# Writing the SSD skip term into the output banks with ScalarE ahead of the products

## The chip, the cores and the metric

One core of a Trainium2 chip. The metric is the device time of one execution in microseconds, and the median over runs is compared. TensorE (PE in the profile) multiplies matrices into PSUM banks of 128 x 512 float32; VectorE (DVE), ScalarE (ACT) and GpSimd (POOL) work elementwise; SyncE (SP) issues most of the transfers.

## The reference

A hybrid decoder layer on 1024 tokens of width 1024, float32: a Mamba-2 SSD branch and a latent-attention branch from one input projection, merged by gates, then a gated feed-forward part. The change is in the SSD mixer. With 32 heads of 64 channels, 4 groups of 8 heads, a state of 128 and chunks of 128 tokens it computes

```python
y_diag = jnp.einsum('bcgls,bcgels,bcsgep->bclgep', scores, decay_in, xc)      # within a chunk
y_off = jnp.einsum('bclgn,cbgepn,bcgel->bclgep', cc, prev, jnp.exp(a_cum))    # from the carried state
...
y = ssd_chunked_scan(xs * dt[..., None].astype(xs.dtype), dt * a, bm, cm)     # y_diag + y_off
y = y + xs * d_skip[:, None]                                                  # the skip term
y = y.reshape(b, l, D_INNER) * jax.nn.silu(z)                                 # the gate
y = rms_norm(y.reshape(b, l, SSD_GROUPS, D_INNER // SSD_GROUPS), ...)
```

## The kernel before

**Stages.** The profile's span begins with the norm and small projections, then attention (to about 703 us), then the SSD stage, the output projections of both branches, the up projection and the down projection. Large products are done three times, as float32r high and low parts (`mm3`, L175 to L177: high x high, high x low, low x high); the operands are split by a ScalarE cast (L153, L146) and a subtraction (L154, L148) on GpSimd or VectorE.

**The SSD stage.** It walks over 4 groups `g` of 8 heads and, within a group, over 8 chunks `c` of 128 tokens. Data lie with channels on partitions: `chan[g]` (tile `xg`) is 128 x 4 x 1024, four blocks `j` of 128 channels (two heads each). For each group:

- `conv_group` projects B, C and x of the group (`conv_tile`: matmuls into `lin` banks, eviction to `craw` by ScalarE at L808, convolution by ScalarE at L810 and three VectorE steps at L812, then silu at L816 and L817). It runs as background work for the next group.
- `ssd_inputs(g, c)` prepares a chunk: transposes of x and B (`xp`, `sp`), the decay matrix `seg` (ScalarE: eight L850, then L852; VectorE L864 multiplies the scores on), `xdt`, `xde` and `bt` (L855, L860, L863), and for c > 0 the decayed C in `abc` (ScalarE L866, VectorE L867).
- `ssd_state(g, c)` forms the chunk's state (`sn`, L874) and carries it on (`st`: GpSimd L879, VectorE L881).
- `ssd_output(g, c)` forms the output transposed in one bank `yp` of 128 x 512: for each block j two products of 64 channels x 128 tokens with `seg` (L891, which start their sums), and for c > 0 two with `st` and `abc` (L896, which add to them). Then it issues the load of the next chunk's gate (`z_load`, tile `zt`, on GpSimd's queue, L796), and VectorE adds the skip term block by block (L903, four of 128 x 128) and multiplies with the gate (L905, 128 x 512). The result stays in place in `chan[g]`.
- `ssd_squares` (L914 to L916) and `ssd_finish` norm the group's channels (`np_`, `grr`) and write them to memory.

**Order.** `ssd_steps` yields in the order: state c, inputs c+1, output c. Between two yields `advance` places a counted number of background steps (each one `mm3`) among TensorE's instructions: the convolution of the next group, the z projections (`z_tiles`, evicted by L329 and L330), in the last group the attention branch's output projection (`mla_tiles`, evicted by VectorE at L1033, with splits of its inputs at L146 and L148). These use two `lin` banks in turn. TensorE keeps the order as written. For ScalarE, VectorE and GpSimd in this stage a list planner sets the order of each engine's queue when the program is built, by the written order and its own estimates of when operands are ready; a few splits are tied behind the instruction written before them (`ordered_split`). On the chip each queue runs in order.

**Buffers.** `yp` and `seg` and `zt` have two buffers each, `abc` three; `xp`, `sp`, `sn` and `np_` one bank each; with the two `lin` banks and two `yp` banks all eight banks are in use. `hds` holds half of `d_skip` per channel; the projected activations carry a factor of two from the form of silu that is used, which the halves take out.

## Time and profile before

| | |
|---|---|
| time, median of 3 runs (lowest to highest) | 2197.95 us (2196.79 to 2203.98) |
| profiled execution: time, span | 2203.12 us, 2201.3 us |
| granted TensorE clock, mean | 0.996 |
| busy: PE, DVE, ACT, POOL | 97%, 66%, 48%, 44% |
| first and last L891 | 803.0, 1242.6 us |

A share of busy time is a mean over stages. In the rows of a group the numbers are count, busy time in us, mean ns of one instruction, and the idle time just before these instructions with what ended it. In a timeline row they are the start, the length in us, the engine, the line, the operation with its tiles, and in brackets the idle time ahead of it and its releaser. A row of a list of waits gives total us, how often, and the longest. A row of stretches gives the length and then each engine's busy time with its instruction count.

### The profile page before, as it was taken

To read this page: it belongs to the slowest core of one execution; us is meant where nothing else is said; L and a number is where in the kernel's file an instruction comes from. 1 tells how busy PE (TensorE), PEld (TensorE's weight loads), DVE (VectorE), ACT (ScalarE), POOL (GpSimd) and SP (SyncE) were. 2 spreads that over 40 slices of the span, in tenths; PEclk is the share of its full clock that TensorE was granted. 3 is DMA by queue.
4 is the path that set the end of the run, shared out by engine and by line. 5 is a ranking of instruction groups with operands and counts; after the bars stand their busy time and mean duration, and the time that the engine had idled before them with its cause. 6 is when DMAs were issued, how large, how long until landed. Compare 5 with 4: busy or idle time off the path is not lost. (4 is left out here: it accounts for less than half of the span.)

```text
span 2201.3 us, 30448 instructions
## 1 busy us (share of the span) xinstructions
PE 2145.3 (97%) x10844; PEld 1713.8 (78%) x10844; DVE 1446.8 (66%) x2567; ACT 1064.3 (48%) x2034; POOL 969.6 (44%) x1049
## 2 busy tenths in 40 slices
PE   8999999999999999999999999999899999999999
PEld 7877776777777887778877787887678888877787
DVE  4466756575664469898877746545876676676762
ACT  5445454555454456656564424324655455554330
POOL 2344424432443237665456311013377777744430
PEclk9999999999999999999999999999999999999999
DMA  4221111111112224645266566542132333248642
GB/s 147 69 69 46 40 53 64 50 35 55 64 48 88 93 82 148 195 151 172 92 229 212 178 224 200 166 161 95 63 119 92 111 105 110 96 138 330 258 158 82
DMA packets 121767, 268.97 MB, mean 122 GB/s; under 512 B 13520, under 2 KB 25744, under 8 KB 121616
## 3 DMA queue, kind: packets, MB, share of 16 engines
q1 hardware_dynamic: 105600, 214.47, 29.0%
q0 software_dynamic: 14528, 49.29, 6.8%
q10 hardware_dynamic: 1488, 3.28, 0.4%
q8 instruction: 85, 1.39, 0.3%
q14 instruction: 66, 0.54, 0.1%
HBM read 201.45 MB, written 65.54 MB: 121 GB/s over the span
## 5 line engine op out<-in xcount | busy, mean ns | idle before, releaser
L175 PE MATMUL lin<-h,whi 128*128 128x512 f32 x1440 | 591.6, 411 | 1.5 <-DVE lt L330 1.5
L177 PE MATMUL lin<-h,wlo 128*128 128x512 f32 x1440 | 563.7, 391 | 0.0
L176 PE MATMUL lin<-h,whi 128*128 128x512 f32 x1440 | 562.4, 391 | 0.0
L175 PEld LDWEIGHTS lin<-h,whi 128*128 128x128 f32 x1440 | 270.6, 188 | 83.9 <-issue 33.8
L177 PEld LDWEIGHTS lin<-h,wlo 128*128 128x128 f32 x1440 | 270.4, 188 | 59.8 <-POOL wlo L154 0.4
L176 PEld LDWEIGHTS lin<-h,whi 128*128 128x128 f32 x1440 | 271.5, 189 | 53.2 <-issue 6.7
L154 POOL TENSOR_TENSOR wlo<-wraw,whi 128x512 fp32r<-128x512 f32 x134 | 193.0, 1458 | 169.3 <-ACT whi L153 165.7
L153 ACT CAST whi<-wraw 128x512 fp32r<-128x512 f32 x232 | 141.1, 619 | 260.0 <-PE lin L176 111.1
L664 POOL TENSOR_TENSOR acc<-acc,e 128x512 f32<-128x512 f32 (+3 forms) x80 | 78.8, 984 | 246.1 <-ACT e L659 223.7
L659 ACT ACTIVATE e<-s 128x512 f32<-128x512 f32 (+1 forms) x192 | 93.3, 492 | 153.7 <-DVE s L657 133.1
L1140 DVE TENSOR_TENSOR xlo<-ur,xhi 128x512 fp32r<-128x512 f32 (+1 forms) x41 | 83.0, 2024 | 60.9 <-ACT xhi L1139 60.9
L154 DVE TENSOR_TENSOR wlo<-wraw,whi 128x512 fp32r<-128x512 f32 x98 | 70.0, 725 | 75.1 <-ACT whi L153 74.7
L850 ACT ACTIVATE seg<-abc,acum 128x128 f32<-128x128 f32 x256 | 80.2, 390 | 47.1 <-PE yp L891 41.0
L175 PE MATMUL dps<-tq,h 128*128 128x512 f32 x242 | 96.8, 400 | 5.8 <-DVE xr L1601 3.5
L176 PE MATMUL dps<-tq,h 128*128 128x512 f32 x242 | 96.9, 400 | 0.8 <-DVE tq L154 0.8
L177 PE MATMUL dps<-tq,h 128*128 128x512 f32 x242 | 96.4, 398 | 0.0
L812 DVE SCALAR_TENSOR_TENSOR xg<-craw,cl,xg 128x1024 f32<-128x1024 f32 x48 | 73.7, 1536 | 27.4 <-ACT xg L810 26.9
L664 DVE TENSOR_TENSOR acc<-acc,e 128x512 f32<-128x512 f32 (+3 forms) x80 | 55.1, 689 | 37.1 <-ACT e L659 36.5
L1216 POOL DMA_DIRECT2D mt<-m_d x16 | 8.6, 539 | 147.1 <-DVE gt L1225 97.1
L154 DVE TENSOR_TENSOR h<-ar,h 128x1024 fp32r<-128x1024 f32 (+1 forms) x35 | 56.4, 1616 | 25.4 <-ACT h L153 25.3
L670 PE MATMUL pv<-e,vt 128*64 128x512 f32 (+3 forms) x384 | 72.9, 498 | 0.0
L629 DVE CUSTOM_DVE_ANT_0 s<-s,negw 128x128 f32<-128x128 f32 (+3 forms) x128 | 62.3, 495 | 13.5 <-PE s L627 13.4
(617 smaller groups left out, 5225.7 us busy)
## 6 DMA issues: line engine op xcount, KB each, us to landing
wraw<-in_w_main SPq DMA_DIRECT2D x112, 256.0 KB
ur<-in_w_up SPq DMA_DIRECT2D x44, 512.0 KB
ar<-f_d SPq DMA_DIRECT2D x34, 512.0 KB
abc<-ac_d POOLq DMA_DIRECT2D x32, 512.0 KB, 5.3
wraw<-in_w_ssd SPq DMA_DIRECT2D x64, 256.0 KB
f_d<-wraw POOLq DMA_DIRECT2D x33, 256.0 KB, 2.4
g_d<-lt SPq DMA_DIRECT2D x32, 256.0 KB
z_d<-lt SPq DMA_DIRECT2D x32, 256.0 KB
```

Of the source, the lines that this page charges most:

```text
L153: S.copy(hi, raw)
L154: (eng or V).tensor_sub(lo, raw, hi.bitcast(F32))
L175: PE.matmul(ps, lhsT=ah, rhs=bh, start=first, stop=False, **more)
L176: PE.matmul(ps, lhsT=ah, rhs=bl, start=False, stop=False, **more)
L177: PE.matmul(ps, lhsT=al, rhs=bh, start=False, stop=last, **more)
L629: V.tensor_tensor_reduce(ps[:, 0:w], ps[:, 0:w], negw[:, 512 - w:512], 1.0, 2 * NEG, ALU.add, ALU.max, nm[:, j, i:i + 1])
L659: S.activation(e[:, c0:512], ps[:, 0:w], AF.Exp)
L664: (V if hd else G).tensor_tensor(accs[hd][:, c0:512], accs[hd][:, c0:512], e[:, c0:512], op=ALU.add)
L670: PE.matmul(pv[hd * 64:(hd + 1) * 64, c0:512], lhsT=vt[:, j, hd * 64:(hd + 1) * 64], rhs=es[hd][:, c0:512], start=first, stop=last)
L812: V.scalar_tensor_tensor(c, raw[:, k:k + T], col(cw + k), c, op0=ALU.mult, op1=ALU.add)
L850: S.activation(seg[:, hd, :], abc[:, hd, :], AF.Relu, bias=acum[:, c, 8 * g + hd:8 * g + hd + 1], scale=-1.0)
L1140: eng.tensor_sub(lo, r, hi.bitcast(F32))
```

## The change

`yp` is now taken at the end of `ssd_inputs`, and ScalarE writes the skip term into it there (x of the chunk times `hds`, four copies of 128 x 128 with a per-partition scale). The products of `ssd_output` no longer start their sums; all of them add to what the bank holds. Three new matmuls of 128 x 512, which do start their sums, write the two `yp` banks in full before the first chunk (the first bank twice). VectorE's four L903 are gone, and its last operation reads the bank and the gate and writes `chan[g]`.

```diff
@@ ssd_inputs
                 V.tensor_tensor(abc, abc, Ct[:, cs].unsqueeze(1).broadcast_to([P, 8, P]), op=ALU.mult)
-            return abc, seg, xdt, xde, bt
+            yp = psy.tile([P, 512], F32, name="yp", bufs=2)
+            for j in range(4):
+                S.activation(yp[:, j * P:(j + 1) * P], xs[:, j, cs], AF.Copy, scale=hds[:, 4 * g + j:4 * g + j + 1])
+            return abc, seg, xdt, xde, bt, yp
@@ ssd_state
-            _, _, _, xde, bt = inp
+            xde, bt = inp[3:5]
@@ ssd_output
-            abc, seg, xdt, _, _ = inp
+            abc, seg, xdt, _, _, yp = inp
             cs = slice(c * P, (c + 1) * P)
-            yp = psy.tile([P, 512], F32, name="yp", bufs=2)
...
-                              rhs=seg[:, hd, :], start=True, stop=c == 0)
+                              rhs=seg[:, hd, :], start=False, stop=c == 0, skip_group_check=True)
...
-                                  rhs=abc[:, hd, :], start=False, stop=True)
+                                  rhs=abc[:, hd, :], start=False, stop=True, skip_group_check=True)
...
-            for j in range(4):
-                V.scalar_tensor_tensor(x[:, j, cs], x[:, j, cs], hds[:, 4 * g + j:4 * g + j + 1],
-                                       yp[:, j * P:(j + 1) * P], op0=ALU.mult, op1=ALU.add)
-            V.scalar_tensor_tensor(x[:, :, cs], zts.pop(0), 0.5, x[:, :, cs], op0=ALU.mult, op1=ALU.mult)
+            V.scalar_tensor_tensor(x[:, :, cs], zts.pop(0), 0.5, yp.rearrange("p (j t) -> p j t", t=P),
+                                   op0=ALU.mult, op1=ALU.mult)
@@ before the loop over the groups
         z_load(0)
+        seeded = [psy.tile([P, 512], F32, name="yp", bufs=2) for _ in range(2)]
+        for i in (0, 1, 0):
+            PE.matmul(seeded[i], lhsT=h[0][0][:, 0, 0:P], rhs=h[0][0][:, 0, :], start=True, stop=True)
```

## Prediction

> **What bounds the kernel now.** I read the page's busy times first, then the stretch 790 to 1262 us, which holds the whole scan, then TensorE's waits in it, then the timelines around each wait.

> ```profile
> span 2201.3 us, 30448 instructions
> PE 2145.3 (97%) x10844; PEld 1713.8 (78%) x10844; DVE 1446.8 (66%) x2567; ACT 1064.3 (48%) x2034; POOL 969.6 (44%) x1049
> ...
> 790.00:1262.00 472.00, 463.51 (x2816) 371.18 (x2815) 392.39 (x625) 269.54 (x518) 261.81 (x242) 1.00 0.51 165
> ...
> PE sn L874 <- DVE bt L863: 4.4, 3, 2.3
> PE np__12753 L955 <- DVE grr L125: 1.8, 1, 1.8
> PE lin L175 <- DVE lt L330: 1.5, 1, 1.5
> PE yp L891 <- DVE seg L864: 0.8, 2, 0.5
> ```

> TensorE is the bound. In the third row the columns behind the length are PE, its weight loads, DVE, ACT and POOL: of 472 us TensorE lacks 472 - 463.51 = 8.5 us, and the four waits add up to the same 8.5 us (4.4 + 1.8 + 1.5 + 0.8). DVE is busy 392 of 472 us (83%), ACT 270 (57%). So whatever the change takes from DVE, it can win 8.5 us here at the most, 0.4% of the time. What follows asks which of the seven waits are made of DVE work that the change removes.

> ```profile
> 889.23 0.44 PE L891 MATMUL yp<-seg,xdt 128*64 128x128 f32 x4 [0.55 <-DVE seg L864]
> ...
> 944.14 1.13 PE L874 MATMUL sn<-xde,bt 128*128 128x512 f32 x2 [0.56 <-DVE bt L863]
> ...
> 985.56 1.12 PE L874 MATMUL sn<-xde,bt 128*128 128x512 f32 x2 [1.55 <-DVE bt L863]
> ...
> 999.79 0.44 PE L891 MATMUL yp<-seg,xdt 128*64 128x128 f32 x4 [0.30 <-DVE seg L864]
> ...
> 1136.98 0.50 PE L175 MATMUL lin<-h,whi 128*128 128x512 f32 x1 [1.49 <-DVE lt L330]
> ...
> 1142.25 1.12 PE L874 MATMUL sn<-xde,bt 128*128 128x512 f32 x2 [2.25 <-DVE bt L863]
> ```

> The seventh, 1.78 us, comes at 1260, behind the last product; I leave it as it is.

> ```profile
> 876.00:889.00 13.00, 12.68 (x84) 10.14 (x82) 13.00 (x19) 6.93 (x13) 6.79 (x5) 1.00 0.33 118
> 932.00:944.00 12.00, 11.59 (x78) 9.18 (x76) 12.00 (x16) 4.24 (x7) 9.42 (x7) 1.00 0.50 177
> 960.00:985.00 25.00, 24.01 (x161) 19.20 (x159) 23.25 (x35) 20.82 (x39) 17.20 (x16) 1.00 0.49 161
> 988.00:999.00 11.00, 11.00 (x78) 9.10 (x77) 11.00 (x18) 5.46 (x12) 4.79 (x5) 1.00 0.17 52
> ...
> 876.00:889.00 13.00, 1.12 (x4) 1.00 0.33 118
> ...
> 988.00:999.00 11.00, 1.29 (x4) 1.00 0.17 52
> ...
> 965.13 1.31 DVE L867 TENSOR_TENSOR abc<-abc,chan 128x1024 f32<-128x1024 f32 x1 [1.65 <-ACT abc L866]
> ...
> 974.60 0.86 DVE L903 SCALAR_TENSOR_TENSOR xg<-xg,hds,yp 128x128 f32<-128x128 f32 x3
> ```

> The first four rows are stretches of all engines, the next two the first and last of the same stretches with L903 alone. Ahead of the first four waits DVE (the number after that of the weight loads) is full: 13.00 of 13, 12.00 of 12, 23.25 of 25, 11.00 of 11. Each stretch has the four L903 of a chunk in it (the third eight). There TensorE waits for a DVE that has too much to do.

> **The change, part by part.**

> DVE: four L903 and one L905 a chunk become one product of 128x512.

> ```profile
> L903 DVE SCALAR_TENSOR_TENSOR xg<-xg,hds,yp 128x128 f32<-128x128 f32 x128 | 36.8, 339 | 10.9 <-PE yp L896 8.7 <-PE yp L891 2.1
> L905 DVE SCALAR_TENSOR_TENSOR xg<-zt,xg 128x512 f32<-128x512 f32 x32 | 25.1, 785 | 0.5
> L1033 DVE SCALAR_TENSOR_TENSOR rb<-rb,lin x10: 673/680/686, 1139.9 to 1254.4; 128x512 f32<-128x512 f32 x10
> ```

> The new product has one operand in SBUF and one in a bank, as L1033 has: 680 ns. Removed 36.8 + 25.1, added 32 x 0.68 = 21.8: DVE gains 40.1 us, 1.25 us a chunk. L905 reads both its operands from SBUF and averages 785 ns, while L1033's ten lie between 673 and 686. [...]

> What of it reaches TensorE: each of the four stretches holds one chunk's skip term and product, so about 1.2 us of relief, since DVE was last idle. The waits of 0.55, 0.56 and 0.30 us go wholly. Of 1.55 us at 985.56 I take 1.2: DVE was idle for 1.65 us ahead of 965.13 (above), and of the two chunks in that stretch only the one with L903 at 974.60 comes after that. Sum: -2.6 us. From both sides: 0, if other DVE work in the planner's order takes the place; -3.0, if all four go.

> The waits at 1136.98 and 1142.25 are of another kind:

> ```profile
> 1135.10 0.62 ACT L153 CAST whi<-wraw 128x512 fp32r<-128x512 f32 x1 [3.38 <-DMA wraw<-in_w_mla]
> ...
> 1136.24 0.69 DVE L330 SCALAR_TENSOR_TENSOR lt<-lt,lin 128x512 f32<-128x512 f32 x1 [8.81 <-ACT lt L329]
> ...
> 1136.86 1.06 ACT L866 ACTIVATE abc<-abc 128x1024 f32<-128x1024 f32 x1
> 1137.98 0.62 ACT L146 CAST h<-lt 128x512 fp32r<-128x512 f32 x1
> ...
> 1139.32 0.68 DVE L148 TENSOR_TENSOR h<-lt,h 128x512 fp32r<-128x512 f32 x1
> ```

> DVE stood idle for 8.81 us there; ACT's queue was held by a weight load, and DVE worked off what had piled up behind it. Nothing of that is removed. Instead the seeds come on ACT between L866 and L146: L146 would end at about 1139.85 and not at 1138.60, L148 start 0.5 us later, and with it the `bt` that TensorE waits for. Term: +0.5 us (0 if the planner puts the seeds behind L146, +1.25 if the whole of them shows).

> ACT: four copies of 128x128 a chunk, SBUF to bank, with a scale from a pointer. The nearest row is L850, also 128x128 and one pointer:

> ```profile
> L850 ACT ACTIVATE seg<-abc,acum 128x128 f32<-128x128 f32 x240 | 75.2, 390 | 41.0 <-PE yp L891 41.0
> ...
> 884.89 1.86 ACT L850 ACTIVATE seg<-abc,acum 128x128 f32<-128x128 f32 x6 [1.33 <-PE yp L891]
> ```

> Six in 1.86 us make 0.31 each, four 1.24 us, 32 chunks 40 us: ACT goes from 57% of the stretch to (269.5 + 40) / 472 = 66%. Cover: the seeds are issued at the end of a chunk's inputs, behind L866, and TensorE needs the bank only with that chunk's products.

> ```profile
> 879.63 1.04 ACT L866 ACTIVATE abc<-abc 128x1024 f32<-128x1024 f32 x1
> ...
> 984.41 1.04 ACT L866 ACTIVATE abc<-abc 128x1024 f32<-128x1024 f32 x1
> ...
> 991.01 0.60 DVE L903 SCALAR_TENSOR_TENSOR xg<-xg,hds,yp 128x128 f32<-128x128 f32 x2
> ...
> 991.13 1.06 ACT L816 ACTIVATE craw<-xg 128x1024 f32<-128x1024 f32 x1 [5.68 <-DVE xg L812]
> ```

> The shortest cover that I found is the chunk with L866 at 879.63 and products at 889.23: 889.23 - 880.67 = 8.6 us for 1.24 us of seeds. So the new wait of TensorE on ACT costs nothing; without that cover it would cost up to 1.24 us a chunk. The seeds also add a wait on ACT: with two `yp` banks, those of chunk c+1 must wait for the product of c-1. The worst case that I found is above: L866 ends at 985.45, the last L903 of two chunks earlier ends at 991.61. Queued behind on ACT are L816 and the evictions L808; but ACT stood idle there for 5.68 us anyway, for the same late DVE. Cost 0; if it weren't covered, TensorE would be short of an output bank of its projections.

> TensorE: three matmuls of 128x512 ahead of the first chunk, and the products of a chunk no longer start their sums.

> ```profile
> 1138.48 0.39 PE L175 MATMUL lin<-h,whi 128*128 128x512 f32 x1
> ...
> 1139.16 0.39 PE L175 MATMUL lin<-h,whi 128*128 128x512 f32 x1
> ...
> L891 PE MATMUL yp<-seg,xdt x512: 272/273/324, 803.0 to 1242.6; 128*64 128x128 f32 x171
> L891 PEldq EVENT_SEMAPHORE  x4: 51/51/51, 889.1 to 1240.2; - x4
> L896 PE MATMUL yp<-abc,st x448: 272/273/273, 815.8 to 1242.8; 128*64 128x128 f32 x150
> ```

> Three matmuls pass in 0.68 us: +0.7 us, in full, since nothing waits there. L891 starts a sum, L896 adds to one, both 273 ns: 0. [...]

> POOL's `zt` load waits for the product of the chunk before, which now ends about 1 us sooner; POOL's queue is no later for it: 0.

> Sum: -2.6 + 0.5 + 0.7 = -1.4 us. The profiled execution took 2203.12 us, so 2201.7 by its own time; the median of the runs, 2197.95, lies 5.2 us (0.23%) below it, more than the whole term, and I forecast 2196.5 for the median. A measurement of this kernel tells 0.3%, 6.6 us, from no change.

> **The rivals.**

> A, the sum above: 2196.5; its own range, with the terms at their ends (-3.0 + 0.7 to 0 + 1.25 + 0.7 + 1.4), is 2195.7 to 2201.3.

> B, DVE's relief reaches much further: all seven waits go, because the planner also places other work differently; -8.5 + 0.7 = -7.8, 2190. For it: DVE is full ahead of four waits. Against: the two largest and the seventh (5.5 of 8.5 us) don't come from a full DVE.

> C, slower: ACT becomes the late engine. Its queue is in order; in the last group of heads weight casts (L153), casts of `at` (L146) and seeds all stand in it, and DVE's L148 and `bt` wait behind L146. If ACT has no slack there, the 1.25 us of each of the group's eight chunks shows: +10 + 0.7, 2208.7. It decides from the point where ACT's idle time within a chunk is under 1.24 us. For it: the 0.5 us above. Against: ACT is 57% busy, and the idle times of it that I saw are 1.3 to 5.7 us. [...]

> D, the relief doesn't arrive: DVE is freed at places where TensorE does not wait, and the waits come back elsewhere; +0.7 to +2 us, 2199.

> **How the numbers follow.** A 0.45, D 0.27, B 0.12, C 0.16. A and D lie within 0.3%. B (2190) is over the bound only when nearly all goes: with some spread, 0.10 faster; C needs two thirds of its price: 0.13 slower; the rest within. Range: from B's side 2189.5, where only its extreme is left out, to 2207, short of C's full price.

> **What would show it.** Right: no L903; L905's successor at about 0.68 us with little spread; DVE busy some 40 us less between 790 and 1262, ACT 40 us more; waits of TensorE for `seg` and `bt` around 889, 944, 985, 1000 gone or small; no wait of TensorE for `yp` on ACT; three matmuls on `yp` at about 790. Wrong: TensorE waiting for seeds or for evictions (`lin` behind ACT), or TensorE's share of the stretch below 463 of 472 us.

## The result and the profile after

The changed kernel takes 2210.75 us in the median (2210.10 to 2215.17, 5 runs), the kernel before 2199.72 us beside it (2196.79 to 2203.98, 5 runs): ratio 1.0053, 95% interval 1.0036 to 1.0070. It is slower by 11 us; forecast were 2196.5 us and a range to 2207.

The profiled execution is the slowest of the five (2215.17 us), 11.8 us of span above the one of before. The page's head, and the rows of the stretch 790 to 1262 and of the waits in it that answer to those of before:

```profile
span 2213.1 us, 30445 instructions
PE 2153.8 (97%) x10847; PEld 1718.8 (78%) x10847; DVE 1403.9 (63%) x2439; ACT 1100.5 (50%) x2162; POOL 954.4 (43%) x1049
...
790.00:1262.00 472.00, 458.97 (x2754) 365.97 (x2753) 343.47 (x471) 297.77 (x628) 245.19 (x241) 0.98 0.50 159
...
PE sn L877 <- DVE bt L863: 10.4, 3, 5.0
PE lin L177 <- POOL wlo L154: 1.9, 1, 1.9
PE xp L840 <- DVE xg L817: 0.7, 1, 0.7
```

DVE is 49 us less busy in the stretch (392.39 to 343.47; part of that is work that now falls behind 1262) and TensorE has become idler: 472 - 458.97 = 13.0 us of waits instead of 8.5. The waits of before at 889, 944, 985 and 1000 are gone, as forecast; not one for `seg` is left. Instead TensorE waits 10.4 us in three places for `bt`, each at the start of a group of heads, and the clock column shows 0.98 instead of 1.00.

The three waits, one for POOL, and the stretches behind them. The column behind the five engines is the granted clock:

```profile
909.08 2.08 PE L877 MATMUL sn<-xde,bt 128*128 128x512 f32 x2 [3.04 <-DVE bt L863]
...
1023.07 1.12 PE L877 MATMUL sn<-xde,bt 128*128 128x512 f32 x2 [2.36 <-DVE bt L863]
...
1153.19 2.07 PE L877 MATMUL sn<-xde,bt 128*128 128x512 f32 x2 [5.02 <-DVE bt L863]
...
1176.96 0.51 PE L177 MATMUL lin<-h,wlo 128*128 128x512 f32 x1 [1.88 <-POOL wlo L154]
...
908.40:915.20 6.80, 6.12 (x12) 4.18 (x13) 2.37 (x4) 0.74 (x2) 3.94 (x3) 0.50 0.48 161
1024.50:1027.90 3.40, 3.40 (x10) 2.63 (x9) 0.25 (x1) 0.52 (x2) 1.80 (x2) 0.50 0.54 177
1150.80:1157.60 6.80, 4.41 (x8) 2.82 (x9) 6.30 (x10) 3.42 (x7) 4.36 (x3) 0.50 0.56 176
1178.10:1181.50 3.40, 3.40 (x10) 2.63 (x9) 1.75 (x2) 0.62 (x1) 1.20 (x2) 0.50 0.76 207
```

At each wait the granted clock is halved for one or two windows of 3.41 us: 6.8 + 3.4 + 6.8 + 3.4 = 20.4 us at half speed. TensorE is busy in 17.3 of them (6.12 + 3.40 + 4.41 + 3.40); the rest is the end of the waits themselves. The 128x512 products into `lin` start 0.43 us apart in them (1025.32, 1025.75, 1026.18), and 0.23 us behind them (1028.13, 1028.36). Half of 17.3, 8.7 us of work, is lost by the granted 0.50, an estimate. Before had no such window in this stretch. The scan's last norm shows the sum, and the two stretches from 790 us to it show the idle time; before, then after:

```profile
L955 PE MATMUL np__12753<-cn,grr x4: 272/273/295, 1260.3 to 1260.7; 128*128 128x128 f32 x4
...
L955 PE MATMUL np__12758<-cn,grr x4: 272/272/294, 1276.1 to 1276.4; 128*128 128x128 f32 x4
...
790.00:1260.30 470.30, 461.82 (x2806) 369.70 (x2805) 391.35 (x623) 269.40 (x518) 261.81 (x242) 1.00 0.51 166
...
790.00:1276.08 486.08, 472.07 (x2816) 376.67 (x2814) 353.75 (x497) 305.03 (x641) 246.08 (x242) 0.98 0.50 161
```

It comes 15.7 us later: 5.5 more of waits (486.08 - 472.07 = 14.0 of idle time against 8.5), 8.7 of clock, 0.7 of new matmuls, and 1.2 by which TensorE is late already where the scan begins (its first L840 starts at 793.5 against 791.6, and 0.7 of that are the new matmuls). The four make 16.1. The 1.2 us have nothing to do with the change as far as is known: in after's execution a half-clock window falls at 502 us, in before's it does not. Behind the norm, where the change touches nothing, after is 3.9 us shorter (936.7 against 940.6 to the end of the span); half-clock windows fall there too (at 1546.7 us in after, at 1533.8 in before), and elsewhere in each execution. Over all runs, span x (1 - mean clock) is 16.8 us in the mean for after and 10.3 for before (35 runs of the second job below). So of the 11 us between the medians at most some 6.5 are clock, since the product also counts half-clock time that lies over a wait and costs nothing; the rest is waits and matmuls.

**Why `bt` is late.** Three rows of before at the second group's start, of ACT and of DVE:

```profile
887.47 1.24 ACT L810 ACTIVATE xg<-craw,cl 128x1024 f32<-128x1024 f32 x1
...
896.85 2.31 DVE L817 SCALAR_TENSOR_TENSOR xg<-craw,xg 128x1024 f32<-128x1024 f32 x1
...
900.31 1.23 DVE L867 TENSOR_TENSOR abc<-abc,chan 128x1024 f32<-128x1024 f32 x1 [0.55 <-ACT abc L866]
```

The same place after, first ACT, then DVE:

```profile
890.88 0.63 ACT L914 ACTIVATE sq__9119<-xg 128x512 f32<-128x512 f32 x1 [3.07 <-DVE xg L904]
891.41 0.57 ACT L808 COPY craw<-lin 128x512 f32<-128x512 f32 x1
...
892.18 1.23 ACT L810 ACTIVATE xg<-craw,cl 128x1024 f32<-128x1024 f32 x1
...
902.41 0.37 ACT L870 ACTIVATE yp<-xg,hds 128x128 f32<-128x128 f32 x1 [0.52 <-DVE xg L817]
902.72 1.26 ACT L850 ACTIVATE seg<-abc,acum 128x128 f32<-128x128 f32 x4
...
905.13 1.04 ACT L866 ACTIVATE abc<-abc 128x1024 f32<-128x1024 f32 x1
...
893.45 3.75 DVE L812 SCALAR_TENSOR_TENSOR xg<-craw,cl,xg 128x1024 f32<-128x1024 f32 x2 [2.67 <-ACT xg L810]
...
900.57 1.80 DVE L817 SCALAR_TENSOR_TENSOR xg<-craw,xg 128x1024 f32<-128x1024 f32 x1 [1.13 <-ACT craw L816]
...
906.21 1.22 DVE L867 TENSOR_TENSOR abc<-abc,chan 128x1024 f32<-128x1024 f32 x1 [3.23 <-ACT abc L866]
...
908.74 0.28 DVE L863 COPY bt<-sp 128x128 f32<-128x128 f32 x1
```

Two delays in ACT's queue add up. First, the planner now reckons the gate's product earlier and has put the squares L914 ahead of L808 and L810 of the next group's last convolution tile. L914 waits 3.07 us for L904, L810 stands behind it (892.18, before 887.47), L812 and L817 follow, and x is ready at 900.57 + 1.80 = 902.4 and not at 899.2. Second, a seed of the new group's first chunk waits for that x (902.41) and, in order, holds back the second chunk's L850 and L866. DVE waits 3.23 us for L866 (before: 0.55), with L863, that is `bt`, behind that wait.

### The profile page after: what moved, and what is told of

The parts are those of the page before. It is cut to its first block, busy times and chain, and to the rows that moved or that the text cites. A ratio compares the mean times of both kernels' runs of the same rounds, so it can differ in the third digit from the quotient of the medians.

```text
span 2213.1 us, 30445 instructions
## 1 busy us (share of the span) xinstructions
PE 2153.8 (97%) x10847; PEld 1718.8 (78%) x10847; DVE 1403.9 (63%) x2439; ACT 1100.5 (50%) x2162; POOL 954.4 (43%) x1049
## 5 line engine op out<-in xcount | busy, mean ns | idle before, releaser
L175 PE MATMUL lin<-h,whi 128*128 128x512 f32 x1440 | 595.1, 413 | 1.0 <-DVE lt L330 1.0
L175 PEld LDWEIGHTS lin<-h,whi 128*128 128x128 f32 x1440 | 272.4, 189 | 85.0 <-issue 34.1
L154 POOL TENSOR_TENSOR wlo<-wraw,whi 128x512 fp32r<-128x512 f32 x134 | 189.5, 1431 | 216.8 <-ACT whi L153 214.8
L153 ACT CAST whi<-wraw 128x512 fp32r<-128x512 f32 x232 | 141.0, 619 | 240.8 <-PE lin L176 111.4
L154 DVE TENSOR_TENSOR wlo<-wraw,whi 128x512 fp32r<-128x512 f32 x98 | 69.0, 716 | 73.7 <-ACT whi L153 73.4
L850 ACT ACTIVATE seg<-abc,acum 128x128 f32<-128x128 f32 x256 | 81.6, 389 | 43.8 <-PE yp L893 36.7
L175 PE MATMUL dps<-tq,h 128*128 128x512 f32 x242 | 97.0, 401 | 5.4 <-ACT h L153 1.9
L812 DVE SCALAR_TENSOR_TENSOR xg<-craw,cl,xg 128x1024 f32<-128x1024 f32 x48 | 77.2, 1608 | 33.9 <-ACT xg L810 33.1
L629 DVE CUSTOM_DVE_ANT_0 s<-s,negw 128x128 f32<-128x128 f32 (+3 forms) x128 | 62.3, 495 | 13.5 <-PE s L627 13.4
L175 PE MATMUL s<-qh,kh 97*128 97x512 f32 (+1 forms) x192 | 68.7, 358 | 1.3 <-ACT qh L644 0.8
```

The source lines that it names most:

```text
L153: S.copy(hi, raw)
L154: (eng or V).tensor_sub(lo, raw, hi.bitcast(F32))
L175: PE.matmul(ps, lhsT=ah, rhs=bh, start=first, stop=False, **more)
L629: V.tensor_tensor_reduce(ps[:, 0:w], ps[:, 0:w], negw[:, 512 - w:512], 1.0, 2 * NEG, ALU.add, ALU.max, nm[:, j, i:i + 1])
L812: V.scalar_tensor_tensor(c, raw[:, k:k + T], col(cw + k), c, op0=ALU.mult, op1=ALU.add)
L850: S.activation(seg[:, hd, :], abc[:, hd, :], AF.Relu, bias=acum[:, c, 8 * g + hd:8 * g + hd + 1], scale=-1.0)
```

## The experiments

Twelve runs of eleven kernels (g2 is f1 once more) in three jobs of the chip; the kernel before ran beside each (medians 2198.69, 2199.91 and 2198.57 us). "Scan" is the start of the last `np` matmul in the profiled execution, "clock" the mean over the runs of span x (1 - granted clock). The profiled executions differ by up to 3.9 us before the scan begins (first L840 at 789.6 us in g2, 793.5 in after), so scan ends closer than that say little.

| kernel | median us | ratio to before, 95% | scan | clock |
|---|---|---|---|---|
| before | 2199.72 | 1 | 1260.7 | 10.3 |
| after | 2210.75 | 1.0053 (1.0036 to 1.0070) | 1276.4 | 16.8 |
| e1 no seeds | 2201.25 | 1.0007 (0.9996 to 1.0017) | 1263.0 | 9.5 |
| e7 first chunk the old way | 2206.63 | 1.0030 (1.0019 to 1.0041) | 1265.1 | 13.4 |
| e5 filler, 7.7 us each | 2220.49 | 1.0090 (1.0074 to 1.0106) | 1277.2 | 11.8 |
| e2 more background ahead | 2209.43 | 1.0040 (1.0025 to 1.0054) | 1270.7 | 13.9 |
| f1, g2 squares later | 2203.17, 2200.17 | 1.0014 (1.0004 to 1.0024), 1.0012 (0.9999 to 1.0026) | g2 1262.8 | 11.0, 9.7 |
| f2 e7 and squares later | 2202.24 | 1.0009 (0.9998 to 1.0019) | 1263.8 | 11.0 |
| f3 e1 and squares later | 2198.52 | 0.9995 (0.9986 to 1.0004) | 1259.3 | 10.0 |
| f4 before, squares later | 2204.93 | 1.0023 (1.0013 to 1.0034) | 1266.4 | 11.4 |
| g1 filler, 2.6 to 5.2 us | 2205.60 | 1.0028 (1.0016 to 1.0041) | 1265.5 | 6.6 |
| e12 first seeds later | 2207.27 | 1.0039 (1.0027 to 1.0052) | 1268.4 | 13.7 |
| f5 e12 and squares later | 2201.60 | 1.0011 (1.0002 to 1.0020) | 1265.1 | 10.8 |

**e1: no seeds.** The skip term is left out, and with it the three matmuls that open the banks.

```diff
-            for j in range(4):
-                S.activation(yp[:, j * P:(j + 1) * P], xs[:, j, cs], AF.Copy, scale=hds[...])
...
-                              rhs=seg[:, hd, :], start=False, ...
+                              rhs=seg[:, hd, :], start=True, ...
```

> The changed kernel without ScalarE's four seeds a chunk and without the three matmuls on `yp`; the products start their sums again, VectorE still multiplies bank and gate in one operation. The skip term is left out of the result. Theory S (the seeds, standing in ScalarE's in-order queue, make TensorE wait at the starts of groups, and waits over some 2 us halve the clock for a few us): the waits for `bt` at the three group starts (3.0, 2.4, 5.0 us) shrink to 4 us together or less, no half clock in 790 to 1262, 2198 us (2195 to 2201). Rival D (the freed VectorE changes the planner's order, the squares L914 come earlier on ScalarE and block it): the waits stay, 2208 to 2212.

Between the medians 9.5 us of the 11 go with the seeds. That is near theory S (2201.25 is just above its range), but its "no half clock" did not come: the last group's wait for `bt` is still 3.44 us, with a half-clock window behind it (the stretch 1130 to 1150 has a clock of 0.91). And the kernel is only level with before, although DVE has 34.5 us less to do in the stretch:

```profile
790.00:1262.00 472.00, 463.67 (x2806) 370.73 (x2804) 357.88 (x493) 267.75 (x517) 243.28 (x242) 1.00 0.49 165
...
PE sn L875 <- DVE bt L863: 4.1, 2, 3.4
PE xp L840 <- DVE xg L817: 3.4, 2, 2.6
```

TensorE's busy time is that of before (463.51). What the lighter DVE gives at 889 to 1000 comes back as waits for x: the squares stand ahead of L808 and L810 here too.

**e7: the first chunk of each group the old way**, the other 28 seeded.

```diff
-            for j in range(4):
+            for j in range(4 if c else 0):
                 S.activation(yp[:, j * P:(j + 1) * P], ...)
...
```

> The changed kernel, but the first chunk of each group the old way: no seeds, its products start the sums of the bank, VectorE adds the skip term block by block. Theory S, narrowed (the first chunk's seeds wait for the new group's x, and hold up L850, L852 and L866 of the second chunk behind them, for which VectorE's L867 waits ahead of `bt`): the waits at the group starts shrink to 4 us together, 2201 us (2198 to 2204). Rival L (ScalarE has too much to do, 40 us of seeds wherever they stand): 28 of 32 chunks still seeded, so 2209 to 2211. Rival D: 2208 to 2212.

Missed by all three forecasts: 2206.63 lies between them. About 4 us come back for four chunks of 32, so a group's first seeds cost more than their share; the other 28 chunks' seeds still cost some 5 us here against e1. On the page ACT is busy 1096.7 us, after 1100.5 with all the seeds.

**e5: a filler ahead of the first state.** 12 matmuls of 128x384 at the start of groups 2 to 4, so that TensorE works where it waited.

```diff
             sn = psx.tile([P, 512], F32, name="sn")
+            if c == 0 and g:
+                for _ in range(12):
+                    PE.matmul(sn[:, 0:NCON], lhsT=ident, rhs=cn, start=True, stop=True)
```

> The changed kernel with twelve matmuls of 128x384 float32 on `sn` ahead of the first state of groups 1 to 3, about 4 us each time, whose results are overwritten: TensorE works in the stretch where it waited. Nothing else gets earlier. Theory C (the waits themselves halve the granted clock for 3.4 to 6.8 us after them): the clock stays 1.00 in the stage, 20.5 us at half speed go (10.2 us), against 1 to 2 us of filler beyond the waits: 2202 us (2200 to 2204). Rival T (the clock is cut for another reason, heat or power, and the waits come with it by chance): half-clock stretches stay, 2211 to 2214.

Missed, by a fault of the experiment: each float32 matmul became two instructions (72 in the trace for 36 written), so a filler took 7.7 us, 23.2 in all against 10.4 us of waits. Even so the scan ends only 0.8 us later than in after: 12.8 us of added work were nearly paid for, by a clock of 1.00 throughout the stretch and by other waits that are gone. The median is still 9.7 us above after's; in the profiled executions most of that lies behind the scan (945.1 us to the end of the span against 936.7), and why is not shown. The cleaner run is g1, below.

**e2: more background work ahead of the group's first state**, eight steps taken from later ones.

```diff
-            advance(8 if g else 14)
-            n = (106, 104, 128, 112)[g]
+            advance(16 if g else 14)
+            n = (106, 96, 120, 104)[g]
```

> The changed kernel with 16 instead of 8 background steps ahead of the first chunk of groups 1 to 3 (8 fewer spread over the rest): 8 x 0.69 = 5.5 us more of TensorE's own work before it asks for the new group's x. Theory S with C: the waits of 3.0 and 2.4 us go, that of 5.0 nearly, the clock stays up: 2199 us (2196 to 2202). Rival L: the lateness comes back in the chunks after, where fewer steps are left, 2207 to 2212.

Missed: within its interval no better than after. The lateness only moved, to the evictions of the background work itself:

```profile
PE lin L175 <- DVE lt L330: 6.8, 2, 3.6
PE yp L893 <- DVE seg L864: 2.8, 2, 1.7
PE sn L877 <- DVE bt L863: 1.4, 1, 1.4
```

Each of the two waits for L330 is followed by half-clock windows (3.11 us at 901 and 3.64 us at 1017; the 128x512 products behind them take 0.63 us, at full clock 0.39). It is ACT's and DVE's queues that are late, and not TensorE that comes too early.

**f1 and g2: the squares later.** The squares of a group's seventh chunk are written together with those of its eighth, and the planner then has L808 and L810 ahead of them.

```diff
-                else:
-                    ssd_squares(g, c - 1)
...
             if half:
+                ssd_squares(g, NT - 2)
                 ssd_squares(g, NT - 1)
```

> The changed kernel with the squares L914 of a group's seventh chunk written later, in `ssd_finish` beside those of the eighth; the planner then has them behind the last L808 and L810 of the next group's convolution on ScalarE, as in the kernel before. Theory Q (with fewer VectorE operations the planner puts these squares ahead of L808 and L810; on the chip they wait up to 3 us there for the gate's product, and the new group's x is late by as much): x is in time at the first two group starts; what stays is the wait that the first chunk's seeds make, 1 to 2.5 us each; half-clock stretches at these two starts mostly go: 2205 us (2202 to 2208). Rival L (ScalarE has too much work in all): 2209 to 2212.

> The changed kernel with only the seventh chunk's squares written later, once more, for a trace of it. Theory queue: no L914 ahead of the last tile's L808 and L810 at the second and third group starts, x from L817 as early as in the kernel before (899 and 1010 us), and the wait of L877 for L863 there shorter than 3.04 and 2.36 us by some 2 us each, under the 2 us at which the clock falls; the wait at the last group start, 5.0 us with L153 in the way, stays. Time 2203, give or take 3. Theory load: the waits of L877 are as before, 2.4 to 3 us, and the gain came from the tail.

Some 8 to 11 us come back, with all seeds in place. f1's profiled execution ran at a clock of 0.18 and left no usable trace; g2 is the same kernel once more:

```profile
889.29 0.35 ACT L870 ACTIVATE yp<-xg,hds 128x128 f32<-128x128 f32 x1
...
893.89 1.80 DVE L817 SCALAR_TENSOR_TENSOR xg<-craw,xg 128x1024 f32<-128x1024 f32 x1 [1.13 <-ACT craw L816]
...
903.54 0.70 PE L877 MATMUL sn<-xde,bt 128*128 128x512 f32 x1 [1.43 <-DVE bt L863]
...
1012.91 1.13 PE L877 MATMUL sn<-xde,bt 128*128 128x512 f32 x2 [0.75 <-DVE bt L863]
```

x is ready at 895.7 instead of 902.4, and the waits for L863 fall from 3.04 and 2.36 to 1.43 and 0.75, by 1.6 us each (2 expected). Neither is followed by a half-clock window (the 128x512 products at 905.65 and 1014.11 take 0.39 and 0.40 us). The last group's, expected unchanged at 5.0, fell to 2.7. But TensorE now waits 3.65 us at 1164 for POOL's L154, and there the scan's one half-clock window stands.

**f2, f3: the same move with e7 and with e1** (f3 leaves the skip term out).

> Both: the first chunk of each group the old way, and the squares of the seventh chunk later. Theory S with Q: no wait over 1 us at the first two group starts, that at the third (3.1 us, a late weight load) stays: 2199 us (2196 to 2202). Rival L: 28 of 32 chunks are still seeded, 2206 or more.

> No seeds (the skip term is left out), and the squares of the seventh chunk later. Theory Q: VectorE's 35 us less now count, the waits for x (0.8 and 2.6 us) and for `bt` and `seg` go: 2196 us (2193 to 2199), below the run without seeds alone. Rival: VectorE's relief brings nothing to TensorE anyway, 2199 to 2202.

f2 adds nothing to f1, and lies just above its range. f3 takes work off DVE and puts none on ACT: 0.9995 of before, not to be told from it, so that its number, in theory Q's range by half a microsecond, does not decide. Its waits do: those for x are gone as theory Q has it, those for `bt` and `seg` are not. They have the same names as before, and nearly the same sum:

```profile
790.00:1262.00 472.00, 464.52 (x2815) 371.76 (x2814) 358.83 (x498) 268.88 (x518) 248.15 (x242) 1.00 0.49 165
...
PE sn L875 <- DVE bt L863: 3.1, 3, 2.2
PE np__12625 L952 <- DVE grr L125: 1.7, 1, 1.7
PE lin L175 <- DVE lt L330: 1.4, 1, 1.4
PE yp L891 <- DVE seg L864: 1.2, 1, 1.2
```

**f4, the control: the move alone, in the kernel before.**

> The kernel before with the squares of the seventh chunk later: the control. All theories: ScalarE's order at the group starts is as before, 2198 to 2201 us.

Missed: slower by 0.23%. The move is no gain in itself. Without the wait of L914 ahead of them ACT's weight casts come 1.5 us sooner (L153 at 890.30, before 891.76), the order of POOL's queue differs too, and POOL's L154 starts at 893.85 instead of 896.34, beside DVE's L812. First a timeline row of DVE, then its L812 by the shortest, median and longest in ns, then two rows of POOL:

```profile
892.16 5.55 DVE L812 SCALAR_TENSOR_TENSOR xg<-craw,cl,xg 128x1024 f32<-128x1024 f32 x2
...
L812 DVE SCALAR_TENSOR_TENSOR xg<-craw,cl,xg x3: 1281/1498/4235, 892.2 to 897.9; 128x1024 f32<-128x1024 f32 x3
...
893.85 2.55 POOL L154 TENSOR_TENSOR wlo<-wraw,whi 128x512 fp32r<-128x512 f32 x2
...
896.91 1.39 POOL L915 TENSOR_TENSOR sq__9243<-sq__9243 128x256 f32<-128x256 f32 x1
```

One L812 takes 4.2 us instead of 1.3 and TensorE waits 1.6 us for `bt` at the start of the second group, where before has no wait. At the last group's start the wait is 2.99 us instead of 2.25, with a half-clock window behind it (0.97 in 1150.8 to 1157.6 us) that before does not have. The L812 of 4.2 us ends at 897.71, so POOL's two L154 (893.85 to 896.40) run beside it; no run isolates what made it long.

**g1: a filler of the waits' own length**, 5, 4 and 8 matmuls.

```diff
-                for _ in range(12):
+                for _ in range((0, 5, 4, 8)[g]):
```

> The changed kernel with 5, 4 and 8 plain matmuls of 128x384 ahead of the first state (L877) of the second, third and last group, so that TensorE works while the first state waits for VectorE's L863. By the filler run that was too long, one such matmul is two instructions of 0.32 us, 0.645 us together, so the three fillers are 3.2, 2.6 and 5.2 us, 11.0 us in all, against waits of 3.04, 2.36 and 5.02 us, 10.4 us in all, in the changed kernel. Theory clock (the waits of 2 us and more cost more than their length, since the granted clock falls to half in the 3.413 us windows behind them, 10.2 us in the stage): the work added lies in the waits, no half-clock window is left in the group starts, and the kernel is 9 to 11 us faster than the changed kernel, near 2201, give or take 4 us for where the half-clock windows of the tail fall. Theory waits (what is lost is the waits alone, and the half clock comes for another reason): nothing is gained, 2210 to 2212.

This is the measurement of the clock by itself: TensorE does 11.0 us of useless work where it waited 10.4.

```profile
790.00:1262.00 472.00, 469.86 (x2830) 374.37 (x2830) 349.75 (x486) 303.13 (x638) 246.55 (x242) 1.00 0.49 164
...
L958 PE MATMUL np__12775<-cn,grr x4: 270/272/274, 1265.2 to 1265.5; 128*128 128x128 f32 x4
```

The clock stays at 1.00 and the scan ends 10.9 us earlier than in after, with nearly as much between its matmuls. Of these, 1.2 us were there before the scan began (first L840 at 792.3 against 793.5); the 9.7 left fit the 8.7 us of clock. Over the runs the clock term falls by 10.2 us (16.8 to 6.6). The median gained only 5.1 us, less than the 9 to 11 expected: the span without the clock term is 3.7 us longer (2196.9 against 2193.2). Some of that is the term itself, which counts half-clock time over waits too (1.5 us in after's profiled scan), and the fillers were cut to the waits of after's slowest execution; for the rest the runs don't say by what. Theory "waits" (no gain) is out: every run of g1 is faster than every run of after.

**e12: the first chunk's seeds behind the second chunk's L866.**

```diff
             inp = abc, seg, xdt, xde, bt
+            if c == 0:
+                return inp
+            if c == 1:
+                first_bank[0] = seed(g, 0)
+            return inp + (seed(g, c),)
...
```

> The changed kernel with all 32 chunks seeded, but the seeds of a group's first chunk written behind the second chunk's L850, L852 and L866 in ScalarE's queue instead of ahead of them (some 15 us of TensorE's work still lie between there and the first chunk's products); the squares stay where they are. Theory queue (the first chunk's four seeds, 1.25 us and a wait for x, hold back the second chunk's L866, and so VectorE's L867 and L863 and TensorE's L877): the waits for L863 at the three group starts shrink to those of the run in which the first chunk was done the old way (0.44 us at the second group, near 3 at the last), and the time is near that run's, 2205 to 2207; the wait for x behind the squares, 2.6 us at two group starts, stays. Theory load (the seeds cost by their sum on ScalarE, wherever they stand): no gain, 2209 to 2212.

As the queue's theory has it: no seed less, and by the medians 3.5 us back, near e7 (the intervals of the two ratios, e12's and after's, overlap, so the time alone does not prove it). The waits say more. Those for L863 at groups 2 and 3 are gone; those for x, made by the squares, stand alone, and the last group's stays:

```profile
PE xp L840 <- DVE xg L817: 4.2, 2, 2.6
PE sn L888 <- DVE bt L863: 3.7, 1, 3.7
```

**f5: the whole change with both moves.**

> The whole change, all 32 chunks seeded, with both reorderings of ScalarE's queue: the first chunk's seeds behind the second chunk's inputs, and the seventh chunk's squares written with the eighth's, behind the last convolution tile's L808 and L810. Theory queue: the waits at the group starts are those of the run with the first chunk the old way and the squares later (0.9, 0.4 and 3.0 us for L863, 1.2 and 1.4 us for L860), and the time 2201 to 2204, level with the kernel before within 0.3%. Theory load: about what the squares alone gave, 2203, with the waits for L863 at the group starts unchanged at 2 to 5 us. That VectorE's 35 us less in the stage come through (2190 to 2196) neither theory expects.

(The wait called L860's in that text is the one for `seg`, L864.) All 32 chunks are seeded by ACT, and the time is 1.0011 of before (1.0002 to 1.0020), no better than with the squares alone.

```profile
PE lin L177 <- POOL wlo L154: 4.4, 3, 3.5
PE sn L888 <- DVE bt L863: 3.7, 3, 2.6
```

Its L863 waits were 0.9, 0.3 and 2.6 us, so it is the waits, and not the time, that speak against theory load. The largest is now the 3.5 us for L154 at 1164, with two half-clock windows behind it (the clock of 790 to 1262 is 0.99): L154 stands in POOL's queue behind a DMA issue (L1040) that itself waited 4.6 us for a store. So the 1.24 us a chunk on ACT cost little once they stand in the right places, some 3.5 us in all by the ratios of f5 and of f3, which has no seeds (1.0011 and 0.9995, with intervals that overlap slightly); and nothing is gained. No kernel of the twelve runs that computes the skip term beats the one before.

## Why the prediction was wrong

The new operations' groups in after:

```profile
L870 ACT ACTIVATE yp<-xg,hds 128x128 f32<-128x128 f32 x128 | 46.2, 362 | 3.6 <-DVE xg L817 2.3
...
L904 DVE SCALAR_TENSOR_TENSOR xg<-zt,yp 128x512 f32<-128x512 f32 x32 | 21.7, 679 | 11.6 <-PE yp L898 9.3 <-PE yp L893 2.3
```

**DVE's relief, -2.6 us: the four waits went, the gain did not come.** L904 takes 679 ns (680 reckoned), and DVE's busy time fell by 42.9 us on the page (40.1 reckoned). All four waits at 889, 944, 985 and 1000 vanished. Not by the relief alone: f3 has the same relief, and waits of 0.66 and 1.23 us at 942 and 997. And the working took the queues' order as fixed, which is the other half of what failed. Its bound "0, if other DVE work in the planner's order takes the place" stopped at zero; the planner moved ACT's L914 too, and with that came waits where there had been none. e1 and f3 show rival D's outcome: 34 us less DVE work, no gain clear of the noise.

**The seeds "cost nothing": the step that failed.** The cover, 8.6 us from L866 to the same chunk's products, was real: TensorE never waits for a seed. What was not asked is who stands behind the seeds in ACT's queue: the next chunk's L850 and L866, whose L867 stands ahead of `bt` in DVE's. At a group's start that chain has no slack, and there a seed also waits for x: TensorE waited 3.04, 2.36 and 5.02 us for `bt` at the three starts, where before had none, none and 2.25. 46.2 us of seeds by their own durations (362 ns each) are no load that ACT could not bear: f5 keeps them all at 1.0011.

**The last group's start, +0.5 us.** The right mechanism, ACT's queue with weight loads in it, and too small: 5.02 us of wait after against 1.49 + 2.25 before, +1.3 us; e1, without seeds, still has 3.4 there. That the same thing would happen at the two earlier group starts, where before has no wait at all, was not seen.

**A wait counted at its length.** This is the missing term of the sum, and the largest: 8.7 us of clock in the profiled scan, at most 6.5 over the runs, against 5.5 us more of waits. The prediction's own sign of being wrong came with it: TensorE busy 458.97 us of the stretch, below 463.

**Right:** the three matmuls (three of 389 ns in 0.7 us); L893 at a median of 273 ns, as L891, with four waits of 51 ns as before. No run shows the 1.4 us at the slow end of A's range: those four waits are all that L893 has. The sum gives POOL no gain; POOL was busy 245.2 us in the stretch instead of 261.8. Rival C came closest in time (2208.7) and named the engine. Its condition, too little idle time of ACT in each chunk of the last group, was not the cause: the loss sits at three group starts and goes with the order.

What stays open: why g1's gain in the median is half of the clock term it removes, what the 28 later seeds cost by, and how much of the spread between f1 and g2 (3 us for one kernel) is the chip.

## What to carry to other kernels

When work moves to an in-order queue, look past its own consumer: list what stands behind it in that queue and who waits for that, above all where a phase begins and the queue's input is itself late. When a planner orders the queues, a shorter operation changes the order of others; compare the orders and not only the durations. Where a matrix engine is busy 97% of the time, price a new wait by the clock behind it as well: here four waits of 12.3 us in all (1.88 to 5.02) had 20.4 us at half clock at and behind them, an estimated 8.7 us of work lost. The waits for `bt` came from two delays, and taking either away, all the seeds (e1) or the squares ahead of x (g2), recovered most of the loss, while moving only the first seeds (e12) recovered a third.
